# Six column groups of a conditioning projection: matmuls on TensorE replaced by product-sums on VectorE

## The chip, the cores and the metric

The kernel runs on one core of a Trainium2 chip. The metric is the device time of one execution in microseconds (us). A core has five engines, each with an instruction queue of its own that it takes in order: TensorE (PE, matrix multiply; PEld is its weight load), VectorE (DVE), ScalarE (ACT), GpSimd (POOL) and SyncE (SP, which here only issues transfers). They wait for each other by semaphores. Sixteen DMA engines move data between DRAM and the core's memory (SBUF); matmul results land in PSUM.

## The reference

One inference step of a two-layer trunk over 128 context tokens and 1024 latent tokens with 1024 features. The even layer runs neighbourhood attention beside a bidirectional gated linear attention (GLA), the odd layer window attention beside a DeltaNet; each layer ends in a convolutional FFN. Every sub-layer is shifted, scaled and gated by numbers that a projection of the conditioning vector gives:

```
def adaln(cond, w, b):
    return jnp.split(jax.nn.silu(cond) @ w + b, 6, axis=-1)
```

`cond` is one vector of 1024 for the context tokens and one for the latent tokens; `w` is 1024 by 6144 for each layer. So 2 x 6144 sums of 1024 products are needed for a layer. Nothing of it depends on the tokens.

## The kernel before

All activations lie with features on the 128 partitions and tokens along the free axis. Products of full precision are made by three passes (the weights and the activations are split into a high and a low part, `whi`, `wlo`, `hh`, `hl`; helper `gemm8`, L156 to L158).

The conditioning projection of the even layer has 6144 columns, that is 12 groups of 512 or 48 chunks of 128. Groups 0 to 3 are made at the start of the kernel, groups 4 to 9 during the linear attention (`even_b`), chunks 40 to 47 and all of the odd layer later on GpSimd and ScalarE (`ada_side`). `ada_groups` makes a group with eight matmuls (L208): silu(cond), 128 x 32, is the stationary side, a 128 x 512 piece of the weights (256 KB, tile `wada`, two buffers in `even_b`) the moving one. ScalarE copies the result (L211, `adarow`), four small matmuls turn it onto the partitions (L215), and VectorE adds the bias (L216).

`even_b` goes through four pairs of heads, p = 0 to 3. For each, `main(p)` runs the chunks of the recurrence: decay factors are multiplied onto keys and queries (L984, `kt` and `qt`, VectorE), each chunk's keys are transposed (L997, `ktr`, PE), copied out of PSUM (L999, `ktok`, VectorE), multiplied with the values (L1017, `u`, PE) and chained (L1005, VectorE); then come the attention inside a chunk (L1049 `att`, L1052, L1053) and the outputs (L1065, L1070 `ob`). Beside it `side(p)` yields the projections for pair p + 1 (`proj_b`, PE), its decay exponents (`zgen`, L910 to L932: `z` on PE, then ScalarE and VectorE) and the conditioning groups. A greedy weave lays them side by side in the program, and the framework's scheduler then sets the final order on each engine; in this part of the kernel no engine's order is written out by hand. Each engine's queue holds its instructions in that one order, transfers issued by SP included.

The line of `side(p)` for p < 3 is

```
yield from self.mix(proj(), self.ada_groups([(0, 4 + 2 * p), (0, 5 + 2 * p)], mp, 2), 1, 1)
```

The results are needed for the gate of the first sub-layer (chunks 16 to 23, when the output projection adds to the rows) and for the FFN's shift and scale (chunks 24 to 39).

Of the kernel before, what the change touches and what calls it, by code (L numbers as in the profile page):

```python
# [8 lines left out]
F32 = mybir.dt.float32  # L9
# [3 lines left out]
ALU = mybir.AluOpType  # L13
# [3 lines left out]
T = 1152  # L17
# [23 lines left out]
NEG = -1.0e30  # L41
# [11 lines left out]
class Net:  # L53
# [42 lines left out]
    def banks(self, g, m):  # L96
        """the banks of PSUM, until the stack is closed"""
        st = ExitStack()
        self.pg = st.enter_context(self.tc.tile_pool(name="pg", bufs=g, space=PSUM))
        self.pm = st.enter_context(self.tc.tile_pool(name="pm", bufs=m, space=PSUM))  # L100
        return st
# [22 lines left out]
    def pat(self):  # L124
        """either kind of bank, in turn"""
        self.turn = (self.turn + 1) % 8
        return self.pgt() if self.turn in (0, 3, 6) else self.pm.tile([128, 512], F32, name="g", tag="m")
# [34 lines left out]
    def proj(self, name, i, blocks, evict):  # L162
        """h @ a chunk of 128 columns; the next chunk of the plan is split meanwhile"""
        key = (name, i)
        if self.plan and self.plan[0] == key:
            self.plan.pop(0)
        if self.ahead is None or self.ahead[0] != key:
            self.ahead = (key, self.wchunk(self.I[name][i]))
        hi, lo = self.ahead[1]
        for b, (c0, n) in enumerate(blocks):  # L170
            ps = self.pgt()
            self.gemm8(ps, hi, lo, self.hh, self.hl, c0, n)
            if b == 0 and self.plan:
                self.ahead = (self.plan[0], self.wchunk(self.I[self.plan[0][0]][self.plan[0][1]]))
            evict(b, ps)
            yield 3.9

    def cond(self):
        nc = self.nc
        s = self.const("cond_s", [128, 8, 2])  # L180
        nc.sync.dma_start(s, self.I["condT"])
        self.nc.scalar.activation(s, s, AF.Silu)
        s4 = self.const("cond_s4", [128, 8, 32])
        nc.gpsimd.memset(s4, 0.0)
        nc.scalar.copy(s4[:, :, 0:2], s)
        self.s4 = s4

    def ada_groups(self, groups, pool, bufs):
        """silu(cond) @ ada_w for 512 columns each, the partial products in four column groups"""
# [13 lines left out]
        for l, g in groups:  # L203
            ps = self.pgt()
            for k in range(8):
                load()
                r = slice(32 * (k % 4), 32 * (k % 4) + 32)
                nc.tensor.matmul(ps[r, :], self.s4[:, k, :], ws.pop(0), start=(k < 4), stop=(k >= 4), skip_group_check=True)  # L208
                yield 0.6
            row = self.spool.tile([128, 512], F32, name="adarow", tag="part", bufs=1)  # L210
            nc.scalar.copy(row, ps)  # L211
            ps = None
            pt = self.pmt()
            for j in range(4):
                nc.tensor.matmul(pt[:, 2 * j:2 * j + 2], row[:, j * 128:(j + 1) * 128], self.sel42, start=True, stop=True)  # L215
            nc.vector.tensor_tensor(  # L216
                out=self.ada[l][:, 4 * g:4 * g + 4, :],
                in0=pt[:, 0:8].rearrange("p (a b) -> p a b", b=2),
                in1=self.adab[l][:, 4 * g:4 * g + 4].unsqueeze(2).to_broadcast([128, 4, 2]),
                op=ALU.add,  # L220
            )
            yield 0.4

    def ada_side(self, parts):
        """silu(cond) @ ada_w with the outputs on the partitions, for chunks of 128 columns: products on GpSimd, sums on ScalarE"""
# [61 lines left out]
    def weave(self, main, fill):  # L287
        """main yields how much of fill (us) to put in next, or None when it waits for fill"""
# [74 lines left out]
    def norm_row(self, x, l, w, b, k, r):  # L363
        """the modulated norm of a row in three steps, to lay between matmuls"""
# [28 lines left out]
    def slot(self, rate):  # L393
        """a step of each row under way, and of as many new ones as the rate says"""
# [8 lines left out]
    def norm_steps(self, b, t0, t1, row):  # L403
        """the norm of a block; its rows are left to slot()"""
# [9 lines left out]
    def blocks(self, x, order, gate, work, post, hook, rate, rate2, pool):  # L414
        """work(b, m) leaves what is to be added to row m of block b; the norm of a block goes on beside the next one's matmuls"""
# [34 lines left out]
    def scaled(self, t, x, l, w, b, k, r):  # L450
        """x over its norm; but for GpSimd's rows, also times the norm's gain and the scale"""
# [8 lines left out]
    def shifted(self, t, l, w, b, k):  # L460
        """plus the shift, in two parts"""
# [47 lines left out]
    def attn(self, mp, units, fill, depth=1):  # L509
        """units yields None (not ready) or a unit; three stages in flight, the first over depth units"""  # L510
# [103 lines left out]
    def even_gate(self, popen, I):  # L614
        """the first norm, modulated by halves of the rows as their shifts and scales come; silu of half of the linear attention's output gate"""
# [221 lines left out]
    def narrow(self, src, dst):  # L837
        """h @ w for 32 columns of w; dst(b, ps) gets [32, n]"""
# [13 lines left out]
    def even_b(self, mp):  # L852
# [48 lines left out]
        def zgen(p):  # L901
            """decay exponents, relative to the middle of each chunk"""
# [191 lines left out]
        def side(p):  # L1094
            if p < 3:
# [6 lines left out]
                yield from self.mix(proj(), self.ada_groups([(0, 4 + 2 * p), (0, 5 + 2 * p)], mp, 2), 1, 1)  # L1102
# [29 lines left out]
    def conv_ev(self, mp, w, dst):  # L1132
        """three-tap convolution; dst [128, T]"""
# [24 lines left out]
    def odd_1(self, mp, zp):  # L1158
# [26 lines left out]
        def gates():  # L1185
            """decay and write strength, per token: partition (head parity, token in chunk)"""
# [140 lines left out]
        def inv(p):  # L1327
            """inverse of the unit triangular 32 by 32 diagonal blocks, one system per partition"""
# [33 lines left out]
        def proj_c(i):  # L1362
            """a chunk for the window attention; but for the values, also with the rotated halves exchanged"""
# [71 lines left out]
    def odd_2(self, mp, zp):  # L1435
# [29 lines left out]
        def merge(p, d):  # L1465
            """inverse of the unit triangular blocks of 64"""
# [126 lines left out]
    def odd_3(self, pp, x):  # L1593
# [73 lines left out]
        def post(cs, small):  # L1667
            """norm and gate of six chunks; returns them by features"""
# [160 lines left out]
    def mix(self, a, b, na, nb):  # L1829
        """na steps of a, then nb of b, and so on"""  # L1830
# [12 lines left out]
    def split_t(self, dst, k, t):  # L1843
        """a row block of the mixers' output, in two parts"""
# [18 lines left out]
    def out_half(self, l, qs, row, then, done=None, later=None):  # L1863
        """output projection of the first mixer: adds to two rows of x for each of qs"""
# [37 lines left out]
    def out_rest(self, l, x, ws, order, hook):  # L1902
        """output projection of the second mixer, and the norm that follows"""
# [13 lines left out]
    def ffn_first(self, l, b, m):  # L1917
        """the first weights of the FFN, ahead of it"""
        j = FG[0][0]
        if (b, m) in ((l ^ 1, 0), (2, 3)):  # L1920
            self.first.append(self.wchunk(self.I["ffnup"][l, 2 * j + 1 - len(self.first)]))

    def ffn(self, l, x, start, hook, side=None, steps=None):
# [3 lines left out]
        with tc.tile_pool(name=f"ffn{l}", bufs=2) as fp:  # L1927
# [87 lines left out]
            def down_block(g, ws, i, b):  # L2015
                """ws: chunks of weights, of which the parts from i on are used"""
# [78 lines left out]
def mask_a():  # L2095
    """additive mask (0 or NEG) of a strip of 8 columns against the strips around it; order (column, row)"""
# [41 lines left out]
def outchunks(w):  # L2138
    """[half of the rows][pair of column blocks][128, (column block, row block, column)]"""
# [185 lines left out]
```

## Time and profile before

| | |
|---|---|
| runs | 3506.6, 3506.62 and 3512.47 us, median 3506.62 |
| span of the profiled execution | 3510.8 us |
| PE busy | 96% of the span |
| DVE, ACT, POOL busy | 56%, 41%, 23% |
| the linear attention's first three pairs | about 458 to 720 us |

The profile gives no time of the profiled execution besides its span, which lies between the lowest and the highest of the runs. Busy time counts instructions that compute; waits and issues of transfers are not in it. PEclk is the granted clock of TensorE as a share of full speed. In a chain of waits each piece is what the next one had to wait for, so a piece's length is time that the end of the kernel hung on.

### The profile page before, as it was taken

The page shows a single profiled execution, that of the slowest core. Times are in us where ns is not written, and L with a number is a line of the kernel's source. Part 1 is how long each engine was busy: PE and PEld are TensorE (multiplying, and loading weights), DVE is VectorE, ACT ScalarE, POOL GpSimd, SP SyncE. Part 2 cuts the span into 40 slices and gives each one's busy share as a digit, 9 for nine tenths or more (in the row PEclk, how much of TensorE's full clock was granted, in tenths as well). Part 3 has the DMA queues.
Part 4 walks back from the last instruction along what each step waited for, and adds up shares of the span by engine and source line. Part 5 has one row for each costly group of instructions (what it writes and reads, how often), then busy time and mean ns, then how long its engine had stood idle before and what let it go on. Part 6 is the DMA issues. An engine that isn't in the chain of part 4 may idle for free.

```text
span 3510.8 us, 58537 instructions
## 1 busy us (share of the span) xinstructions
PE 3355.3 (96%) x23239; PEld 3074.0 (88%) x23239; DVE 1975.3 (56%) x3848; ACT 1432.3 (41%) x3265; POOL 802.3 (23%) x1064
## 2 busy tenths in 40 slices
PE   6999999999999999999899877999999999999997
PEld 4988777779999999999798776677889999999997
DVE  5354444456655555555757776655676454445556
ACT  4355444444644444443554444541254222212223
POOL 1000010002544544451306676002310000000002
PEclk9999999999999999999999988999999999999999
DMA  5211122243222222221213454206511111111111
GB/s 197 85 49 49 54 62 84 84 161 129 77 84 80 83 76 86 82 88 52 84 57 106 123 135 131 52 15 205 164 46 29 41 42 41 41 44 43 43 43 66
DMA packets 182523, 282.04 MB, mean 80 GB/s; under 512 B 81867, under 2 KB 126027, under 8 KB 182124
## 3 DMA queue, kind: packets, MB, share of 16 engines
q1 hardware_dynamic: 151084, 224.88, 20.7%
q10 hardware_dynamic: 27184, 38.68, 3.8%
q0 software_dynamic: 3984, 14.75, 1.5%
q8 instruction: 184, 3.01, 0.4%
q14 instruction: 87, 0.71, 0.1%
HBM read 229.89 MB, written 48.37 MB: 79 GB/s over the span
## 4 chain that ended last, share of the span: by engine, by line
PE 81%; POOL 6%; DMA 4%; DVE 4%; ACT 2%; issue 2%; SPq 1%; DVEq 0%; POOLq 0%; ACTq 0%
PE g L156 14%; PE g L157 14%; PE g L158 14%; PE g L2025 5%; PE g L2023 5%; PE g L2024 5%; PE g L1860 4%; POOL sysN L1357 3%; POOL syst L1355 2%; PE s L507 2%; PE s L506 2%; PE ptr L595 2%; PE pvo L606 2%; PE g L208 2%; PE kqs L1631 1%
## 5 line engine op out<-in xcount | busy, mean ns | idle before, releaser
L156 PE MATMUL g<-hh,whi 128*128 128x386 f32 (+2 forms) x3264 | 1123.2, 344 | 18.6 <-ACT df L1373 11.2
L157 PE MATMUL g<-hl,whi 128*128 128x386 f32 (+2 forms) x3264 | 1113.5, 341 | 1.7 <-DVE hl L389 1.7
L158 PE MATMUL g<-hh,wlo 128*128 128x386 f32 (+2 forms) x3264 | 1109.2, 340 | 5.2 <-DVE wlo L144 5.1
L156 PEld LDWEIGHTS g<-hh,whi 128*128 128x128 f32 x3264 | 620.3, 190 | 41.0 <-issue 20.2
L157 PEld LDWEIGHTS g<-hl,whi 128*128 128x128 f32 x3264 | 619.3, 190 | 10.8 <-issue 6.8
L158 PEld LDWEIGHTS g<-hh,wlo 128*128 128x128 f32 x3264 | 618.7, 190 | 7.0 <-DVE wlo L144 5.9
L1933 ACT ACTIVATE u<-g,cw 128x384 f32<-128x384 f32 (+1 forms) x264 | 153.9, 583 | 769.8 <-PE g L158 769.8
L1934 DVE SCALAR_TENSOR_TENSOR u<-g,cw,u 128x384 f32<-128x384 f32 (+1 forms) x264 | 163.2, 618 | 528.9 <-ACT u L1933 528.6
L481 DVE SCALAR_TENSOR_TENSOR x<-g,ada,x 128x128 f32<-128x128 f32 (+1 forms) x608 | 294.7, 512 | 205.3 <-PE g L2025 190.9
L141 ACT CAST whi<-wraw 128x1024 fp32r<-128x1024 f32 (+2 forms) x202 | 201.1, 995 | 459.3 <-PE g L2024 238.7
L2024 PE MATMUL g<-gl,whi 128*128 128x384 f32 (+1 forms) x1008 | 341.4, 339 | 1.9 <-DVE gl L1989 1.9
L2023 PE MATMUL g<-gh,whi 128*128 128x384 f32 (+1 forms) x1008 | 342.7, 340 | 0.2
L2025 PE MATMUL g<-gh,wlo 128*128 128x384 f32 (+1 forms) x1008 | 342.4, 340 | 0.0
L144 DVE TENSOR_TENSOR wlo<-wraw,whi 128x1024 fp32r<-128x1024 f32 (+2 forms) x214 | 256.2, 1198 | 118.8 <-ACT whi L141 118.6
L262 POOL TENSOR_TENSOR adat<-wada,adas 128x384 f32<-128x384 f32 x168 | 174.7, 1040 | 318.9 <-DMA wada<-in_adaw 279.1
L2024 PEld LDWEIGHTS g<-gl,whi 128*128 128x128 f32 x1008 | 190.8, 189 | 2.4 <-issue 2.4
L262 POOL TENSOR_TENSOR wada<-wada,adas 128x384 f32<-128x384 f32 x168 | 189.0, 1125 | 13.2
L2023 PEld LDWEIGHTS g<-gh,whi 128*128 128x128 f32 x1008 | 190.7, 189 | 0.8 <-issue 0.8
L2025 PEld LDWEIGHTS g<-gh,wlo 128*128 128x128 f32 x1008 | 189.9, 188 | 0.0
L1970 POOL MEMSET gh<- 128x1 f32 x44 | 4.3, 100 | 782.0 <-PE g L2025 777.5
L1935 DVE SCALAR_TENSOR_TENSOR u<-g,cw,u 128x384 f32<-128x384 f32 (+1 forms) x264 | 163.3, 619 | 9.3
L1860 PE MATMUL g<-hh,whi 128*128 128x384 f32 (+1 forms) x384 | 117.1, 371 | 10.5 <-DVE x L481 4.7
(363 smaller groups left out, 4952.6 us busy)
## 6 DMA issues: line engine op xcount, KB each, us to landing
wraw<-in_ffnup SPq DMA_DIRECT2D x88, 512.0 KB
wada<-in_adaw ACTq DMA_DIRECT2D x112, 192.0 KB
wada<-in_adaw SPq DMA_DIRECT2D x80, 256.0 KB
wraw<-in_wi SPq DMA_DIRECT2D x38, 512.0 KB
kq<-kq_dram SPq DMA_DIRECT2D x36, 512.0 KB
wraw<-in_ffndn SPq DMA_DIRECT2D x40, 384.0 KB
wada<-in_adaw ACTq DMA_DIRECT2D x56, 128.0 KB
wraw<-in_wi ACTq DMA_DIRECT2D x12, 512.0 KB
```

Of the source, the lines that this page charges most:

```text
L141: nc.scalar.copy(hi[:, :n], raw[:, :n])
L144: nc.vector.tensor_tensor(out=lo[:, c], in0=raw[:, c], in1=hi[:, c].bitcast(F32), op=ALU.subtract)
L156: mm(ps[:, :n], w, ah[:, k, c0:c0 + n], start=(k == 0), stop=False)
L157: mm(ps[:, :n], w, al[:, k, c0:c0 + n], start=False, stop=False)
L158: mm(ps[:, :n], lo[:, k * 128:(k + 1) * 128], ah[:, k, c0:c0 + n], start=False, stop=(k == 7))
L262: nc.gpsimd.tensor_tensor(out=d[:, :m], in0=w[:, :m], in1=sb[:, j, sl], op=ALU.mult)
L481: nc.vector.scalar_tensor_tensor(out=xr[:, t:t + nn], in0=ps[:, o:o + nn], scalar=gate[:, m, j:j + 1], in1=xr[:, t:t + nn], op0=ALU.mult, ...
L1860: mm(ps[:, :n], a[:, w], src[:, 2 * k + j, c0:c0 + n], start=(k + x == 0), stop=(k + x == 5))
L1935: nc.vector.scalar_tensor_tensor(out=t, in0=ps[:, 2:n], scalar=w[:, 2:3], in1=t, op0=ALU.mult, op1=ALU.add)
L2023: mm(ps[:, :n], hi[:, o:o + 128], gh[:, c0:c0 + n], start=(s == 0), stop=False)
L2024: mm(ps[:, :n], hi[:, o:o + 128], gl[:, c0:c0 + n], start=False, stop=False)
L2025: mm(ps[:, :n], lo[:, o:o + 128], gh[:, c0:c0 + n], start=False, stop=(s == ng - 1))
```

## The change

Groups 4 to 9 (chunks 16 to 39) are made by `ada_rows` on VectorE: one instruction multiplies a 128 x 512 piece of the transposed weights (outputs on the partitions, half of the 1024 inputs along the free axis) with silu(cond), spread over all partitions, and adds up the products into one number per partition. Each piece is used twice, for the two conditioning vectors; the second time the products overwrite the piece. Eight chunks go with each pair of heads: first their first halves, then their second. The weights' buffers stay at two. silu(cond) goes to DRAM at the start and comes back spread (`csb`, 512 KB for each half, one buffer). Three small tiles change their pool.

```diff
     def cond(self):
         nc = self.nc
-        s = self.const("cond_s", [128, 8, 2])
+        s = self.gp.tile([128, 8, 2], F32, name="cond_s", tag="cond_s", bufs=1)
         nc.sync.dma_start(s, self.I["condT"])
         self.nc.scalar.activation(s, s, AF.Silu)
-        s4 = self.const("cond_s4", [128, 8, 32])
+        self.cs_dram = self.dr.tile([1, 2, 1024], F32, name="cs_dram")
+        for j in range(2):
+            nc.scalar.dma_start(self.cs_dram[0, j].rearrange("(k p) -> p k", p=128), s[:, :, j])
+        s4 = self.gp.tile([128, 8, 32], F32, name="cond_s4", tag="cond_s4", bufs=1)
...
+    def ada_rows(self, l, c0, c1, pool):
+        nc = self.nc
+        n = c1 - c0
+        todo = [(c, h) for h in range(2) for c in range(c0, c1)]
+        ws = []
+
+        def load():
+            if todo:
+                c, h = todo.pop(0)
+                w = pool.tile([128, 512], F32, name="wada", tag="wada", bufs=2)
+                nc.sync.dma_start(w, self.I["adaw2"][l, c, :, 512 * h:512 * h + 512])
+                ws.append(w)
+
+        load()
+        acc = pool.tile([128, 8, 2, 2], F32, name="adacc", tag="adacc", bufs=1)
+        for h in range(2):
+            sb = pool.tile([128, 2, 512], F32, name="csb", tag="csb", bufs=1)
+            nc.sync.dma_start(sb, self.cs_dram[:, :, 512 * h:512 * h + 512].to_broadcast([128, 2, 512]))
+            for c in range(n):
+                load()
+                w = ws.pop(0)
+                for j in range(2):
+                    t = pool.tile([128, 512], F32, name="adj", tag="adj", bufs=1) if j == 0 else w
+                    nc.vector.tensor_tensor_reduce(out=t, in0=w, in1=sb[:, j], scale=1.0, scalar=0.0,
+                                                   op0=ALU.mult, op1=ALU.add, accum_out=acc[:, c, j, h:h + 1])
+                yield 0.0
+        out = self.ada[l][:, c0:c1, :]
+        nc.vector.tensor_tensor(out=out, in0=acc[:, :n, :, 0], in1=acc[:, :n, :, 1], op=ALU.add)
+        nc.vector.tensor_tensor(out=out, in0=out, in1=self.adab[l][:, c0:c1].unsqueeze(2).to_broadcast([128, n, 2]), op=ALU.add)
+        yield 0.0
...
-                yield from self.mix(proj(), self.ada_groups([(0, 4 + 2 * p), (0, 5 + 2 * p)], mp, 2), 1, 1)
+                yield from self.mix(proj(), self.ada_rows(0, 16 + 8 * p, 24 + 8 * p, mp), 1, 2)
```

How the instructions stand. First VectorE where the recurrence of pair 0 begins: `wlo` is the low part of the next projection's weights, `qt` the queries, `ktok` the copies of the first two chunks' transposed keys. Before:

```order
L144 TENSOR_TENSOR wlo_4332<-wraw_4329,whi_4331 128x1024
L984 TENSOR_TENSOR qt_4294<-qt_4294,qf_3965 128x1152
L984 TENSOR_TENSOR qt_4296<-qt_4296,qf_3965 128x1152
L999 COPY ktok_4383<-ktr_4380 128x256
L999 COPY ktok_4388<-ktr_4385 128x256
```

And the same place now (the product-sums and the reads of their accumulator both show as ISA, `adacc` holds the sums):

```order
L251 ISA adacc_4346 128x1
L144 TENSOR_TENSOR wlo_4335<-wraw_4332,whi_4334 128x1024
L1019 TENSOR_TENSOR qt_4297<-qt_4297,qf_3968 128x1152
L1019 TENSOR_TENSOR qt_4299<-qt_4299,qf_3968 128x1152
L251 ISA adj_4721,adacc_4346<-wada_4716,csb_4595 128x512
L251 ISA adacc_4346 128x1
L251 ISA wada_4716,adacc_4346<-wada_4716,csb_4595 128x512
L251 ISA adacc_4346 128x1
L255 TENSOR_TENSOR ada0_93<-adacc_4346 128x16
L256 TENSOR_TENSOR ada0_93<-ada0_93,adab0_91 128x16
L1034 COPY ktok_4395<-ktr_4392 128x256
L1034 COPY ktok_4400<-ktr_4397 128x256
```

All 16 pieces of chunks 16 to 23 stand ahead of the first `ktok`, the last one between `qt` and `ktok`. The same place on PE, before (`g` is a projection's result, `ktr` the transposed keys, `u` the product that needs the first `ktok`):

```order
L997 MATMUL ktr_4380<-ident_73,kt_4295 128x128
L997 MATMUL ktr_4380<-ident_73,kt_4297 128x128
L997 MATMUL ktr_4385<-ident_73,kt_4295 128x128
L997 MATMUL ktr_4385<-ident_73,kt_4297 128x128
L208 MATMUL g_4343<-wada_4344,cond_s4_119 32x512
L156 MATMUL g_4413<-hh_131,whi_4236 128x384
L157 MATMUL g_4413<-hl_135,whi_4236 128x384
L1017 MATMUL u_4390<-vtb_3968,ktok_4383 64x64 x4
```

And now:

```order
L1032 MATMUL ktr_4392<-ident_73,kt_4298 128x128
L1032 MATMUL ktr_4392<-ident_73,kt_4300 128x128
L1032 MATMUL ktr_4397<-ident_73,kt_4298 128x128
L1032 MATMUL ktr_4397<-ident_73,kt_4300 128x128
L156 MATMUL g_4419<-hh_134,whi_4239 128x384
L157 MATMUL g_4419<-hl_138,whi_4239 128x384
L158 MATMUL g_4419<-hh_134,wlo_4240 128x384
L1052 MATMUL u_4402<-vtb_3971,ktok_4395 64x64 x4
```

The conditioning matmul is gone, and `u` still stands three matmuls behind the transposes. Last, VectorE ahead of pair 1's first `ktok`, before (`wlo`, `qt` and `ktok` as above):

```order
L144 TENSOR_TENSOR wlo_5015<-wraw_5012,whi_5014 128x1024
L984 TENSOR_TENSOR qt_4977<-qt_4977,qf_4300 128x1152
L984 TENSOR_TENSOR qt_4979<-qt_4979,qf_4300 128x1152
L999 COPY ktok_5086<-ktr_5083 128x256
L999 COPY ktok_5091<-ktr_5088 128x256
```

And now, the end of a run of product-sums that begins right behind `qt` (`oTb` is pair 0's output):

```order
L251 ISA adacc_5771 128x1
L251 ISA wada_5823,adacc_5771<-wada_5823,csb_5772 128x512
L251 ISA adacc_5771 128x1
L998 SCALAR_TENSOR_TENSOR oTb_4669<-oTb_4669,bng_3879,rsb_5091 128x1152
L251 ISA adj_5915,adacc_5771<-wada_5828,csb_5772 128x512
L251 ISA adacc_5771 128x1
L251 ISA wada_5828,adacc_5771<-wada_5828,csb_5772 128x512
L251 ISA adacc_5771 128x1
L251 ISA adj_5920,adacc_5771<-wada_5913,csb_5772 128x512
L251 ISA adacc_5771 128x1
L1034 COPY ktok_5152<-ktr_5149 128x256
L1034 COPY ktok_5157<-ktr_5154 128x256
```

These are product-sums of chunks 32 to 39, which the program yields beside pair 2's projections: they moved ahead of pair 1's recurrence.

## Rows read from the trace of the kernel before

**Rows 1.** The page's head and its busy time by engine.

```profile
span 3510.8 us, 58537 instructions
...
PE 3355.3 (96%) x23239; PEld 3074.0 (88%) x23239; DVE 1975.3 (56%) x3848; ACT 1432.3 (41%) x3265; POOL 802.3 (23%) x1064
```

**Rows 2.** Table by stretch: length, busy us (instructions) by engine, clock, DMA share, GB/s.

```profile
458.00:554.00 96.00, 95.71 (x616) 72.10 (x615) 42.90 (x73) 43.15 (x84) 8.80 (x10) 1.00 0.25 70
554.00:640.00 86.00, 85.87 (x552) 61.73 (x551) 37.10 (x68) 42.76 (x80) 7.47 (x10) 1.00 0.27 82
640.00:720.00 80.00, 79.87 (x517) 55.44 (x516) 34.01 (x68) 39.65 (x79) 7.47 (x10) 1.00 0.32 98
sum 262.00, PE 261.44 PEld 189.26 DVE 114.00 ACT 125.55 POOL 23.75; mean PE 87.15 PEld 63.09 DVE 38.00 ACT 41.85 POOL 7.92
```

**Rows 3.** Chain of waits, 430 to 720 us, shares by line.

```profile
by line: PE g L156 16.9%; PE g L157 16.3%; PE g L158 15.8%; PE g L208 14.2%; PE att L1049 6.2%; PE z L910 5.9%; PE ob L1070 5.1%; PE u L1017 3.6%; PE ob L1065 3.6%; PE ktr L997 2.9%; DMA wada<-in_adaw 2.7%; PE m L215 1.7%; PE vtr L895 1.4%;
```

**Rows 4.** Pieces of that chain: start us, us, engine, tile, line, count.

```profile
469.91 0.98 PE g L208 x2
...
477.27 0.38 PE u L1017 x8
...
512.25 1.05 PE m L215 x8
...
563.33 0.38 PE u L1017 x8
...
594.27 0.79 PE m L215 x8
...
604.87 3.88 DMA wada<-in_adaw
```

**Rows 5.** PE by line, 455 to 715 us: busy us, mean ns, idle before.

```profile
L208 PE MATMUL g<-wada,cond_s 128*32 128x512 f32 x96 | 46.0, 605 | 0.3
...
L215 PE MATMUL m<-sel,adarow 128*128 128x2 f32 x48 | 5.8, 244 | 0.3 <-ACT adarow L211 0.3
```

**Rows 6.** VectorE by line and shape, whole span; columns as in rows 5.

```profile
L561 DVE CUSTOM_DVE_ANT_0 sc<-s,bias 128x512 f32<-128x512 f32 x48 | 33.1, 690 | 42.2 <-PE s L507 41.7
...
L2087 DVE SCALAR_TENSOR_TENSOR x<-x,fing,rb 128x384 f32<-128x384 f32 x14 | 13.9, 1017 | 4.1 <-ACT rb L346 4.1
...
L561 DVE DVE_READ_ACCUMULATOR2_ANT mx<- 128x1 f32 x144 | 11.9, 83 | 0.0
...
L963 DVE SCALAR_TENSOR_TENSOR oTb<-oTb,bng,rsb 128x1152 f32<-128x1152 f32 x3 | 4.3, 1420 | 6.2 <-ACT rsb L962 6.2
```

**Rows 7.** VectorE in order of time, 452 to 500 us; idle before in brackets.

```profile
466.62 1.23 DVE L144 TENSOR_TENSOR wlo<-wraw,whi 128x1024 fp32r<-128x1024 f32 x1 [5.24 <-ACT whi L141]
467.76 2.62 DVE L984 TENSOR_TENSOR qt<-qt,qf 128x1152 f32<-128x1152 f32 x2
475.57 0.76 DVE L999 COPY ktok<-ktr 128x256 f32<-128x256 f32 x2 [5.18 <-PE ktr L997]
```

**Rows 8.** Chain of waits, 0 to 100 us: the first conditioning load.

```profile
16.42 3.21 DMA wada<-in_adaw
```

**Rows 9.** Table by stretch behind a wait of PE, columns as in rows 2.

```profile
736.00:740.00 4.00, 0.47 (x2) 0.50 (x3) 4.00 (x7) 1.07 (x2) 0.00 (x0) 0.84 0.72 224
740.00:744.00 4.00, 4.00 (x14) 4.00 (x14) 2.35 (x4) 1.25 (x2) 0.00 (x0) 0.50 0.47 192
744.00:748.00 4.00, 4.00 (x30) 3.29 (x30) 2.86 (x7) 0.52 (x2) 0.00 (x0) 0.81 0.52 147
```

**Rows 10.** ScalarE in order of time at the start.

```profile
17.41 0.22 ACT L182 ACTIVATE cond_s<-cond_s 128x16 f32<-128x16 f32 x1
```

**Rows 11.** Table by stretch at the start, columns as in rows 2.

```profile
20.00:30.00 10.00, 9.43 (x30) 2.69 (x28) 1.38 (x8) 0.48 (x1) 1.66 (x2) 0.94 1.01 358
```

**Rows 12.** Transfers, 2200 to 2300 us: packets, MB, share of 16 engines.

```profile
DMA packets 8572, 4.60 MB, mean 46 GB/s; under 512 B 7792, under 2 KB 7792, under 8 KB 8560
...
q1 hardware_dynamic: 8560, 4.43, 18.5%
```

More of the change, by code (lines that the diff above doesn't have):

```diff
@@ L209, in ada_groups @@
                 yield 0.6
-            row = self.spool.tile([128, 512], F32, name="adarow", tag="part", bufs=1)
+            row = self.gp.tile([128, 512], F32, name="adarow", tag="part", bufs=1)
             nc.scalar.copy(row, ps)
```

## Prediction

> **What bounds the kernel now.** Read first the page's busy line [rows 1]: TensorE (PE) is busy 96% of the 3510.8 us, VectorE (DVE) 56%. An average does not say what one stage is worth, so next comes the table by stage [rows 2], cut where the kernel goes from one pair of heads of the linear attention to the next: in its three stretches of 96, 86 and 80 us PE is busy 95.71, 85.87 and 79.87 us, at granted clock 1.00, and DVE only 42.90, 37.10 and 34.01. The chain of waits for the same part [rows 3] runs almost wholly over PE: an instruction taken off PE here is time off the end, as long as nothing makes PE wait instead. The pieces of that chain [rows 4] give what one costs: a conditioning matmul (L208, two passes) holds PE for 0.98 us, the eight passes of the small transposes that close a group (L215) for 1.05, elsewhere down to 0.79.
>
> **What is removed.** 48 conditioning matmuls of 0.975 us are 46.8 us, six closing transposes at about 0.85 are 5.1: 51.9 us of PE, which is the whole possible gain. The count agrees with the grouped rows, 96 passes and 48 passes [rows 5]. The six copies of the row on ScalarE and the six small adds on DVE go too and end nothing. The chain also lists 3.88 us of a load at 604.87; PE was working meanwhile (its stage was 85.87 of 86 us busy), so I give nothing for it.
>
> **What is added on DVE.** 24 column chunks in two halves are 48 pieces of 256 KB; each piece gets two product-sums of 128x512. The trace has this instruction with the same shape, in the first mixer's softmax: 690 ns plus 83 ns for the read of the accumulator [rows 6]. There one source lies in PSUM; here both lie in SBUF. Lower bound 0.62 us (the 83 ns and the tail lie under what follows), upper bound from the dearest row with two SBUF sources, 1017 ns for 384 elements, so 1.36 us for 512 [rows 6]. I take 0.77, nearest the row of the same instruction: 1.55 us a piece, 74 us in all. DVE has 262 − 114 = 148 us idle in the three stretches, so the work fits; the order decides whether it fits where it stands. [...]
>
> **Where it stands.** All 16 pieces of the first third come ahead of the first ktok copies in DVE's order, the next 16 and five and a half of the last third ahead of the second stage's ktok copies. So the work runs about a stage earlier than the matmuls did, and DVE is full up to about 570 us. PE needs ktok for its u matmuls, and DVE takes its queue in order.
>
> First ktok. Before, DVE did wlo at 466.62 and qt at 467.76 and then stood idle until PE's ktr released ktok at 475.57 [rows 7]: 5.24 us of idle time ahead of wlo and 5.18 ahead of ktok, 10.4 us in all. Now five pieces (7.7 us) stand there. Of these, one waits for its load: two buffers mean that a piece's load starts when the piece two ahead is done, 3.88 us to landing [rows 4] (3.21 at the start of the kernel [rows 8]), less the 1.55 us of the piece between: 2.3. Further up, the second half of the vector silu(cond) goes into a single buffer, so its load starts only after the last product-sum of the first half; with product-sums queued ahead of the decay steps, kt comes some 5 us late. 5 + 7.7 + 2.3 − 10.4 is 4.6, and PE arrives 1 us sooner without its L208 at 469.91: PE waits 5 to 8 us for ktok, at u (477.27 before).
>
> Second ktok. From the first to the second, DVE has its own 37.5 us (37.10 in 86 us [rows 2], over 87 us), 43 product-sums (33 us), seven places where a third piece follows two with little between (1.65 to 2.35 us each, 12 to 16 us) and one reload of silu(cond) (3.2 to 3.9 us): 86 to 90 us, starting 5 to 8 us after 475.6. That is 567 to 574. PE's u stood at 563.33 [rows 4]. I take 7 us late, and 2 to 14 as ends, since some of the load waits may lie under waits that DVE has anyway, or add to them. So the 18.3 us that PE had been relieved of by then (17 matmuls, two closings) are lost, and 7 more.
>
> From there on. 31 matmuls and four closings are still to go: 30.2 + 3.4 = 33.6 us. Product-sums left: 21, 16 us of DVE in a stage that has 37 us of its own against some 69 of PE (86 less 17), and none in the stage after. I charge 6 us (3 to 10): about 3 for att and z evictions queued behind product-sums, and 3 for the clock. [...] The last stage I charge 1 us.
>
> **The start.** Two stores of silu(cond) to DRAM are put on ScalarE's queue right after the silu at 17.41 [rows 10], each of 1,024 runs of four bytes. From 20 to 30 us the DMA engines are full (1.01) [rows 11] with the loads PE's first matmuls need, and the stores take two of the eight completion semaphores through which SP's loads go in turn, so an early load can wait for a store. A stretch of 8,572 packets, 7,792 of them under 512 bytes, took 18.5% of 16 engines over 100 us for its main queue [rows 12]: 35 ns of an engine each, so 2,048 packets are 4.5 us of all 16. Bounds 0 (under other loads) and 6 us; I take 3. Each reload of the vector is 512 KB, 3 MB in all, in stretches with DMA share 0.25 to 0.32: hidden but for the waits counted.
>
> **Sum.** 33.6 − 7 − 6 − 1 − 3 = 16.6, say 17 us. Taken from the profiled span of 3510.8 it gives 3494; that execution's span lies 4 us above the median of the runs, 3506.6, from which I take it: 3490.
>
> **Rivals.**
> The cover holds everywhere. If DVE is nowhere late, only the start is charged: 51.9 − 3 = 49, so 3458. For it: 148 us of idle DVE. Against: in-order waits for loads with two buffers, and 21 pieces ahead of one needed copy. Chance 0.08.
>
> Slower: product-sums from two SBUF sources run as the 1017 ns row does, at 1.36 us. This adds 0.67 us each: 10 ahead of the first ktok (6.7 us), 43 ahead of the second (29 us), and about 3 us in the third stage, where DVE then has 72 us against PE's 69. 39 − 17 = 22 us slower, 3529. It decides from about 0.98 us a product-sum on, where the 17 us are used up. Against: the 1420 ns row and the 690 ns row. Chance 0.12. [...]
>
> No change: relief given back. The second ktok 14 us late, 12 us lost in the third stage to evictions behind product-sums, the start 6: 33.6 − 33 is nothing, 3506. For it: the same interleaving stands in each stage. Chance 0.18.
>
> That the change would not take the matmuls off PE is excluded by the order of its instructions.
>
> **How the numbers follow.** My forecast has 0.62; with its own ends (second ktok 2 to 14, third stage 3 to 10, start 0 to 6) it covers 3478 to 3504. About 0.2%, 7 us, is what a measurement can tell from no change. Some 0.09 of the forecast lies within that of 3506.6. Faster: 0.53 + 0.08 = 0.61. Same: 0.09 and 0.13 of the third rival, 0.22. Slower: 0.12 and 0.05 of the third rival, 0.17. The range that leaves 2 in 10 outside reaches into both sides: 3470 to 3516.
>
> **What would show it.** Right: no L208 in these stages; the product-sum near 690 ns; PE waiting 5 to 8 us at the first ktok and several at the second, with a granted clock of 0.50 behind; DVE waiting for wada loads some 2 us at a time; no such waits in the last stage, which is about 20 us shorter than before; the first conditioning matmuls about 3 us later. Wrong: a product-sum above 0.98 us, a first u not later than its matmuls allow, or a stage after the second ktok in which PE waits more than 10 us.

## The result and the profile after

The changed kernel takes 3488.48 us (median of 4 runs, 3488.36 to 3488.96), the kernel before 3508.41 us (4 runs, 3506.6 to 3512.47): ratio 0.9932, 95% interval 0.9913 to 0.9952, so 17 to 31 us faster. 3490 us had been predicted. The medians differ by 19.9 us and the two profiled spans by 3510.8 - 3485.9 = 24.9 us: before's span is longer than three of its four run times, so its profile shows the slowest of them, and some 5 us of the 24.9 may belong to that choice of run and not to the change. The head of the changed kernel's page, which answers to [rows 1]:

```profile
span 3485.9 us, 58431 instructions
...
PE 3321.6 (95%) x23095; PEld 3074.4 (88%) x23095; DVE 2035.4 (58%) x4040; ACT 1427.7 (41%) x3259; POOL 810.3 (23%) x1064
```

TensorE (PE) is busy 33.7 us less, not the 51.9 that were taken from it, and VectorE (DVE) 60.1 us more. Where the rest went is seen in a table by stage. The cuts are the first z matmul, the first ktok copy of each of the four pairs, and the last ob matmul. First before, then after (columns: stretch, its length, PE busy with its instructions, granted clock, DMA share, GB/s):

```profile
425.40:475.60 50.20, 50.20 (x268) 1.00 0.14 44
475.60:562.60 87.00, 86.71 (x558) 1.00 0.24 69
562.60:649.20 86.60, 86.47 (x556) 1.00 0.27 83
649.20:740.40 91.20, 85.21 (x542) 0.97 0.44 140
740.40:796.40 56.00, 56.00 (x428) 0.95 0.38 127
```

```profile
433.90:484.70 50.80, 49.72 (x269) 1.00 0.39 122
484.70:569.00 84.30, 78.84 (x532) 0.92 0.34 109
569.00:645.50 76.50, 74.28 (x502) 0.91 0.24 76
645.50:717.30 71.80, 68.00 (x466) 0.90 0.35 115
717.30:773.70 56.40, 55.70 (x431) 0.97 0.43 146
```

Three things stand in these rows. The first z comes 8.5 us later: the start is dearer than it was. The whole stretch is 31.2 us shorter (339.8 against 371.0). And the granted clock, 1.00 in the first two stages of before, is 0.92, 0.91 and 0.90: PE waits little, but part of what is left to it runs at a lower granted clock, 0.50 where it is lowest (528 to 532 us, in the slices below). The stretch is split below into PE's idle time, its clock loss (PE busy times one minus the granted clock, summed over 60 equal slices) and the work at full clock that is left. Work fell from 360.0 to 305.6 us, so the relief of 51.9 was there; idle rose from 6.4 to 13.2, clock loss from 4.6 to 20.9. A stretch of low clock is called a dip below.

**The start.** In the changed kernel SyncE's queue (SP) waits for the two small stores, and the DMA engines, full in before [rows 11], stand mostly idle meanwhile. Its longest wait from 14 to 50 us (who waits, for what: us in total, times, longest):

```profile
SPq L201 <- DMA cs_dram<-cond_s: 10.9, 1, 10.9
```

In the traces of both kernels SP's issues up to 26 us carry eight semaphores in all, and from the ninth on each waits for the transfer that last carried its own. The two stores, issued at 17.74 and 18.16 us, carry two of these eight. SP's next load carries the first store's: the issue before it ends at 18.05, that store's last signal comes at 28.94, and the load is issued at 28.96. Issuing its first sixteen weight loads took 10.10 us before (first line) and takes 19.77 now:

```profile
16.42 10.10 SPq L198 DMA_DIRECT2D wada<-in_adaw  x16
16.67 19.77 SPq L201 DMA_DIRECT2D wada<-in_adaw  x16
```

The stretch of [rows 11] now (the last two columns are the DMA share and GB/s):

```profile
20.00:30.00 10.00, 5.82 (x9) 1.06 (x9) 0.52 (x3) 0.48 (x1) 0.00 (x0) 0.85 0.20 24
```

The stores' own packets are cheap. From 14 to 50 us their queue has 2,080 packets, which took 3.7% of the 16 engines' time, 1.3 us of all sixteen:

```profile
q10 hardware_dynamic: 2080, 0.01, 3.7%
```

**The product-sums** (duration in ns, least, median and most):

```profile
L251 DVE DVE_READ_ACCUMULATOR2_ANT adacc<- x96: 72/81/87, 428.8 to 626.1; 128x1 f32 x96
L251 DVE CUSTOM_DVE_ANT_0 adj<-wada,csb x48: 674/685/985, 428.2 to 624.8; 128x512 f32<-128x512 f32 x48
L251 DVE CUSTOM_DVE_ANT_0 wada<-wada,csb x48: 665/691/1142, 429.0 to 625.5; 128x512 f32<-128x512 f32 x48
```

685 and 691 ns with both sources in SBUF, against 690 for the same instruction with other operations (add and maximum) and one source in PSUM [rows 6]. VectorE's busy time rose by 60.1 us with the 96 of them, 0.63 each: in a row they start as little as 0.61 us apart.

**The waits of PE** from 420 to 800 us:

```profile
PE u L1052 <- DVE ktok L1034: 8.0, 5, 2.1
PE ob L1100 <- POOL at L1088: 2.5, 2, 1.6
PE z L945 <- DVE E L947: 1.1, 1, 1.1
PE vtr L930 <- DVE at L1087: 1.0, 1, 1.0
```

8.0 us of them, in five waits, are for ktok, the kind that was forecast, though each is short. The first is the one ahead of the first u (start, duration, idle before):

```profile
485.18 0.45 PE L1052 MATMUL u<-vtb,ktok 128*64 128x64 f32 x8 [1.57 <-DVE ktok L1034]
```

The others are new: PE waits for GpSimd's and VectorE's steps of the attention and of the decay, where before, with conditioning matmuls in between, it waited for none of these. Behind some of these waits the clock fell, here to 0.50. The second half of the first stage, in slices of 4 us:

```profile
516.00:520.00 4.00, 4.00 (x46) 1.00 0.53 197
520.00:524.00 4.00, 3.45 (x24) 1.00 0.37 131
524.00:528.00 4.00, 3.00 (x16) 0.67 0.16 57
528.00:532.00 4.00, 4.00 (x24) 0.50 0.38 129
532.00:536.00 4.00, 4.00 (x20) 0.55 0.05 17
```

From 528 to 536 PE is busy all the time at about half its clock, after waits of 0.2, 0.3 and 1.1 us from 521 to 525. What PE ran from 515.5 to 531.5 us, grouped by line (count, busy, mean ns, idle before):

```profile
L1084 PE MATMUL att<-qt,kt 64*128 64x128 f32 x38 | 5.0, 314 | 0.2 <-DVE at L1087 0.2
L1105 PE MATMUL ob<-qt,ss 64*64 64x128 f32 x32 | 3.5, 357 | 0.0
L945 PE MATMUL z<-glr,wz 33*128 33x384 f32 x6 | 3.1, 606 | 1.1 <-DVE E L947 1.1
L1100 PE MATMUL ob<-at,vtb 128*64 128x128 f32 x20 | 2.7, 358 | 0.0
L930 PE MATMUL vtr<-ident,vfb 128*128 128x128 f32 x9 | 2.0, 340 | 0.3 <-ACT vtb L931 0.3
L158 PE MATMUL g<-hh,wlo 128*128 128x384 f32 x1 | 0.3, 332 | 0.0
```

One projection matmul (`g`) in 16 us; the rest are short ones or ones on part of the array. In before, the same steps of the attention (502.5 to 518.5 us) had projection and conditioning matmuls among them, and the clock stayed at 1.00:

```profile
L1049 PE MATMUL att<-qt,kt 64*128 64x128 f32 x32 | 3.4, 285 | 0.0
L157 PE MATMUL g<-hl,whi 128*128 128x384 f32 x9 | 3.1, 345 | 0.0
...
L208 PE MATMUL g<-wada,cond_s 128*32 128x512 f32 x4 | 2.1, 604 | 0.0
```

The gaps ahead of this fall are waits for VectorE and ScalarE, the longest of 1.1 us. Such a gap alone does not decide: at the first ktok of this kernel PE waited 1.6 us among projection matmuls, and the clock stayed at 1.00 from 480 to 492; it fell behind the next wait, of 1.9 us, to 0.83 from 492 to 496 and 0.74 from 496 to 500.

**The second ktok.** VectorE's instructions from 562 to 570 us (start, duration, what ended the idle time before):

```profile
562.22 0.69 DVE L251 CUSTOM_DVE_ANT_0 wada<-wada,csb 128x512 f32<-128x512 f32 x1
562.84 0.08 DVE L251 DVE_READ_ACCUMULATOR2_ANT adacc<- 128x1 f32 x1
565.67 1.42 DVE L998 SCALAR_TENSOR_TENSOR oTb<-oTb,bng,rsb 128x1152 f32<-128x1152 f32 x1 [2.74 <-ACT rsb L997]
567.00 0.69 DVE L251 CUSTOM_DVE_ANT_0 adj<-wada,csb 128x512 f32<-128x512 f32 x1
...
568.96 0.75 DVE L1034 COPY ktok<-ktr 128x256 f32<-128x256 f32 x2
```

and the same place before:

```profile
562.61 0.76 DVE L999 COPY ktok<-ktr 128x256 f32<-128x256 f32 x2 [8.24 <-PE ktr L997]
565.18 1.42 DVE L963 SCALAR_TENSOR_TENSOR oTb<-oTb,bng,rsb 128x1152 f32<-128x1152 f32 x1 [1.81 <-ACT rsb L962]
```

VectorE was not full here. It stood for ScalarE's rsb, with ktok queued behind oTb and three product-sums; before, ktok stood ahead of oTb. In the third stage it waits 9.6 us so. From the first to the second ktok VectorE was busy for 65.90 of 84.30 us, and of its idle time only this was for the loads of the product-sums (pieces, then silu(cond)):

```profile
484.70:569.00 84.30, 65.90 (x154) 0.92 0.34 109
DVE adj L251 <- DMA wada<-in_adaw: 4.4, 5, 1.3
DVE adj L251 <- DMA csb<-cs_dram: 2.4, 1, 2.4
```

### The profile page after: what moved, and what is told of

Same layout as the page of the kernel before. It is cut to its first block, busy times and chain, and to the rows that moved or that the text cites. A ratio compares the mean times of both kernels' runs of the same rounds, so it can differ in the third digit from the quotient of the medians.

```text
span 3485.9 us, 58431 instructions
## 1 busy us (share of the span) xinstructions
PE 3321.6 (95%) x23095; PEld 3074.4 (88%) x23095; DVE 2035.4 (58%) x4040; ACT 1427.7 (41%) x3259; POOL 810.3 (23%) x1064
## 4 chain that ended last, share of the span: by engine, by line
PE 79%; POOL 6%; DVE 5%; DMA 3%; issue 3%; ACT 2%; SPq 1%; DVEq 0%; POOLq 0%; ACTq 0%
PE g L156 14%; PE g L157 14%; PE g L158 14%; PE g L2060 5%; PE g L2058 5%; PE g L2059 5%; PE g L1895 4%; POOL sysN L1392 3%; POOL syst L1390 2%; PE s L542 2%; PE s L541 2%; PE ptr L630 2%; PE pvo L641 2%; PE kqs L1666 1%; PE g L1518 1%
## 5 line engine op out<-in xcount | busy, mean ns | idle before, releaser
L156 PE MATMUL g<-hh,whi 128*128 128x386 f32 (+2 forms) x3264 | 1126.8, 345 | 18.4 <-ACT df L1408 12.8
L156 PEld LDWEIGHTS g<-hh,whi 128*128 128x128 f32 x3264 | 623.3, 191 | 32.3 <-ACT df L1408 13.1
L297 POOL TENSOR_TENSOR wada<-wada,adas 128x384 f32<-128x384 f32 x168 | 190.1, 1132 | 13.2
```

The lines of the kernel that those rows point to most:

```text
L156: mm(ps[:, :n], w, ah[:, k, c0:c0 + n], start=(k == 0), stop=False)
L297: nc.gpsimd.tensor_tensor(out=d[:, :m], in0=w[:, :m], in1=sb[:, j, sl], op=ALU.mult)
```

## The experiments

Two theories of where the rest of the 51.9 us went. **A**: VectorE loses it; its product-sums and their loads make ktok late, and the stores the start. **B**: the removed matmuls were themselves the cover for the attention's waits (the work that PE did meanwhile), and the long matmuls among short ones that kept the clock up. On the three chips of the experiments the kernel before ran from 3501 to 3534 us, more widely than on the first, so the lengths from the profiles carry the reading, and the ratio to before on the same chip stands beside them. Lengths in us; "stretch" is first z to last ob.

| kernel | first z | stretch | PE idle | clock loss | ratio to before, 95% |
|---|---|---|---|---|---|
| before | 425.4 | 371.0 | 6.4 | 4.6 | 1 |
| changed | 433.9 | 339.8 | 13.2 | 20.9 | 0.9932 (0.9913 to 0.9952) |
| late_stores | 438.4 | 336.5 | 14.5 | 15.9 | 0.9923 (0.9901 to 0.9945) |
| stores_behind | 422.4 | 333.2 | 11.5 | 16.2 | 0.9901 (0.9874 to 0.9928) |
| before_stores | 436.2 | 370.6 | 6.4 | 4.4 | 1.0034 (1.0020 to 1.0049) |
| relief_only | 420.6 | 332.7 | 8.0 | 19.7 | 0.9871 (0.9828 to 0.9913) |
| relief_spread | 422.2 | 313.5 | 6.9 | 2.6 | 0.9837 (0.9816 to 0.9859) |
| before_spread | 420.3 | 371.4 | 9.0 | 4.0 | 1.0007 (0.9993 to 1.0021) |
| spread | 433.3 | 331.0 | 15.8 | 10.6 | 0.9911 (0.9884 to 0.9938) |
| both | 422.0 | 332.3 | 15.7 | 12.2 | 0.9891 (0.9866 to 0.9916) |
| early_ktok | 424.6 | 329.9 | 15.4 | 8.9 | 0.9885 (0.9864 to 0.9906) |
| one_sum | 436.7 | 340.4 | 14.4 | 21.5 | 0.9951 (0.9930 to 0.9971) |
| w3_inplace | 433.0 | 336.9 | 13.2 | 17.3 | 0.9945 (0.9926 to 0.9964) |
| mix11 | 435.0 | 343.1 | 31.7 | 6.0 | 0.9958 (0.9938 to 0.9978) |

The changed kernel, late_stores and stores_behind have the same instructions in this stretch, and it took 339.8, 336.5 and 333.2 us: with product-sums, differences under some 7 us in one profile are not read. The kernel before, before_stores and before_spread lie within 0.8 us of each other. Each length is from one profile; the ratios of most kernels overlap.

**late_stores.**

```diff
...
-        for j in range(2):
-            nc.scalar.dma_start(self.cs_dram[0, j]..., s[:, :, j])
+        self.cs = s
...
     def even_gate_rest(self):
...
+            self.nc.scalar.dma_start(self.cs_dram[0, p - 2]..., self.cs[:, :, p - 2])
```

> The changed kernel, but the two stores of silu(cond) are issued some 60 us later, after the first conditioning groups, beside the last two chunks of the output gate. Theory A: these stores are what makes the first weight loads late, and all of the 8.5 us by which the changed kernel reaches its first linear-attention projection later (433.9 against 425.4 us); then 3488.5 - 8.5 = 3480 us, and PE's first conditioning matmuls stand where they stood before. Theory B: the delay comes from the other places in memory of the vector and its padded copy, or from the order at the start; then 3488 us, within 2.

It tested nothing: the scheduler put the stores back at 17.5 us, and the first z was as late as before the edit, or later (438.4). Written later is not issued later; inside the stretch whose order is written out by hand it is (the next one).

**stores_behind.**

```diff
...
-        for j in range(2):
-            nc.scalar.dma_start(self.cs_dram[0, j]..., s[:, :, j])
+        self.cs = s
...
                         nc.sync.dma_start(self.br_dram[i], ts[i])
+            for j in range(2):
+                nc.scalar.dma_start(self.cs_dram[0, j]..., self.cs[:, :, j])
             ps = ts = ws = None
```

> The changed kernel with the two stores of silu(cond) behind the first two output gates on ScalarE's queue, where they are held by the order written out by hand (in the first try they were still issued at 17.5 us). Theory A (a store's completion holds back the weight loads behind it): SP issues its first 16 weight loads in about 10 us, as before (19.8 in the changed kernel), the first z matmul comes at 425 us in place of 433.9, and the time is 3488.5 - 8.5 = 3480 us. Theory B (other places in memory, other order): first z at 434, 3488 us.

As theory A had it. The first z came at 422.4, 11.5 us earlier, and the median was 3479.28 us; the interval of its ratio overlaps that of the changed kernel, so the time alone would not show it. The sixteen issues are short again:

```profile
16.46 9.66 SPq L200 DMA_DIRECT2D wada<-in_adaw  x16
```

**before_stores**, the same from the other side.

```diff
         self.nc.scalar.activation(s, s, AF.Silu)
+        self.cs_dram = self.dr.tile([1, 2, 1024], F32, name="cs_dram")
+        for j in range(2):
+            nc.scalar.dma_start(self.cs_dram[0, j]..., s[:, :, j])
```

> The kernel before with the two stores of silu(cond) at the start and nothing else; nobody reads them. If the stores hold back the weight loads behind them, SP takes about 20 us for its first 16 weight loads (10.1 before), the first z comes 8 to 13 us later than 425.4, and the time is 8 to 11 us above before's. If the delay in the changed kernel came from elsewhere, no difference.

The stores alone make the first z 10.8 us late and the time 0.34% longer (12 us; 7 to 17 by the interval), with the same wait in SP's queue:

```profile
SPq L201 <- DMA cs_dram<-cond_s: 13.1, 2, 12.1
```

So the cost of the start is settled: some 8 to 13 us of SP's loads queued behind a store of 4 KB. Over the fourteen profiles the first z stands at 420.3 to 425.4 us in the seven without early stores and at 433.0 to 438.4 in the seven with them.

**relief_only.**

```diff
-                yield from self.mix(proj(), self.ada_groups([(0, 4 + 2 * p), (0, 5 + 2 * p)], mp, 2), 1, 1)
+                yield from proj()
...
+        nc.gpsimd.memset(self.ada[0][:, 16:40], 0.0)
```

> The kernel before with the six groups left out and nothing put in their place: the conditioning values of column groups 4 to 9 are set to zero, so the output is not the reference's. Theory A (VectorE loses the rest): without product-sums PE keeps the whole 51.9 us, 3508.4 - 51.9 = 3456.5 us, the recurrence is 52 us shorter than before (the changed kernel: 32). Theory B (the removed matmuls were themselves the cover for other waits, for POOL's and ScalarE's steps of the attention, and the clock falls behind such waits): the recurrence is shorter by about the same 32 us as in the changed kernel, and without stores at the start the time is 3476 us; the clock is low at the same two or three places.

Theory A alone falls by the profile. With no product-sum and no store the stretch is 38.3 us shorter, not 52, and the clock loss is 19.7 us, as large as in the changed kernel. The time alone would not say so: by the interval it is 31 to 60 us shorter. Theory B had expected 32, so both are tested further. PE's busy time over the whole stretch, and the granted clock:

```profile
420.60:753.30 332.70, 324.74 (x2200) 0.94 0.21 69
```

**spread** lays long matmuls among the short ones.

```diff
+            pq = self.proj("wi0", 12 + p, IB, evict(qf, 0.125))
             for g in range(3):
+                yield next(pq)
                 pt = self.pmt("vtr")
...
-            yield from self.proj("wi0", 12 + p, IB, evict(qf, 0.125))
+            for _ in pq:
+                pass
```

> The changed kernel with one edit in the order: each of the three groups of transposes of v (vtr) comes behind a block of the q projection (24 full matmuls) in place of all three ahead of it, so that long matmuls lie among the short ones of the attention (att, ob, z, vtr) in the second half of each stage. Product-sums and loads stay. Theory B (the rest is lost to the clock, which falls where the removed matmuls had been the only long ones): the 21.0 us of clock loss in the recurrence fall to 5 to 10, 3488.5 - 13 = 3475 us. Theory A (VectorE's queue): waits for ktok stay at 8 us and the time at 3488 us, within 3.

Half as expected. The clock loss fell from 20.9 (16 in the two profiles with the same stretch) to 10.6, but idle rose to 15.8, among it 5.9 us in the third stage for an hh copy of ScalarE that had been hidden. Long matmuls nearby did not always keep the clock up: behind a wait of 1.1 us it stood at 0.50 for some 9 us, in which PE ran 14 projection matmuls.

```profile
534.00:538.00 4.00, 4.00 (x22) 0.50 0.32 113
538.00:542.00 4.00, 4.00 (x13) 0.50 0.17 63
```

The median is 3483.6 us, and the ratio's interval overlaps those of the kernels without the edit.

**relief_spread**, the same edit without product-sums.

> The kernel before with the six groups left out (their values set to zero, the output is not the reference's) and the transposes of v dealt out between the blocks of q. No product-sum, no store. If the 19.7 us of clock loss that the kernel without the groups shows come from stretches that hold only short matmuls, they fall to 10 us or less here, and the recurrence (first z to last ob) from 332.7 to about 322 us. If the clock falls for another reason (waits alone, or the chip at that moment), it stays near 20 us and 333 us.

The clock loss is gone:

```profile
422.20:735.70 313.50, 306.62 (x2198) 0.99 0.22 74
```

19.2 us less than without the edit (332.7), all but 2 of them clock. The whole relief is there: 371.0 - 313.5 = 57.5 us. The median is 3456.56 us. So with the projection's matmuls dealt out among the short ones the clock no longer fell (loss 2.6 us, 19.7 without the edit). Which of theory B's two halves does it is not shown: ahead of the fourth pair's ktok relief_only has 4.9 us of waits for steps of the attention and the decay, and here they are gone as well, so the clock may have stayed up because the waits were covered.

**before_spread.**

> The kernel before with only the transposes of v dealt out between the blocks of q; its conditioning matmuls stay. If the removed matmuls were what kept the clock up in the second half of the stages, nothing is to be had here: clock loss stays near 4.6 us and the time at before's, within 4 us. If the order of the transposes were a gain by itself, 8 to 10 us below.

No difference in time or stretch; clock loss 4.0. The edit has no worth of its own: it does for the kernel without the groups what their matmuls had done.

**one_sum.**

```diff
-                for j in range(2):
-                    t = pool.tile([128, 512], ..., tag="adj", bufs=1) if j == 0 else w
+                for j in range(1):
+                    t = w
...
```

> The changed kernel with one of the two product-sums of each piece: the second batch gets the first's value, so the output is not the reference's. All loads stay. 48 product-sums less are 37 us of VectorE. Theory A (VectorE's queue is what makes PE wait): about half of the 20 us that are lost in the recurrence come back, 3478 us. Theory B (cover lost on PE): 3488 us, within 3, with PE's waits at the same places.

37 us less on VectorE brought nothing that can be measured. VectorE's waits for the pieces grew from 8.0 us to

```profile
DVE wada L251 <- DMA wada<-in_adaw: 25.3, 16, 4.6
```

What a piece with one sum cost ahead of a ktok copy was here largely its load, up to 4.6 us: PE's longest wait for ktok was 6.4 us.

**w3_inplace.**

```diff
-                w = pool.tile([128, 512], F32, name="wada", tag="wada", bufs=2)
+                w = pool.tile([128, 512], F32, name="wada", tag="wada", bufs=3)
...
```

> The changed kernel with three buffers for the pieces in place of two; for their room the first product-sum writes over its piece, and the second reads that, so the output is not the reference's. Theory A: the 8.0 us that VectorE waits for pieces go, and with them up to 5 us of PE's waits for ktok: 3484 us. Theory B: these waits lie where VectorE waits for ScalarE anyway, or the clock decides: 3488 us, within 2.

Not told apart. VectorE's waits for pieces fell from 8.0 to 2.4 us, PE waits 7.7 us for ktok in place of 8.0, and the stretch of 336.9 us lies within what the same kernel shows.

**mix11.**

```diff
-                    yield from self.mix(pr, zgen(p + 1), 1, 2)
+                    yield from self.mix(pr, zgen(p + 1), 1, 1)
```

> The changed kernel with the decay steps of the next pair dealt out one for each block of the projection in place of two. They end behind the q projection. Theory B (clock): z matmuls lie farther apart, clock loss falls from 21.0 us by about 8; the decay of the second direction comes some 10 us later, of which a few us may show as a wait at the next stage's first kt: 3480 to 3488 us. Theory A (VectorE late): the decay steps now end closer to the ktok copies, so waits for ktok grow by 5 us or more at each stage: 3500 us.

The clock loss fell to 6.0 as theory B had it, and was paid for elsewhere, more dearly than theory B said: idle rose by 18.5 us. The time is near theory A's 3500 us, but not by its way: the waits for ktok are 9.2 us in place of 8.0. The decay steps end too late, and PE waits for kt.

```profile
PE ktr L1032 <- DVE kt L1019: 16.9, 3, 11.6
```

In the middle of the second stage PE waited 1.5 us among short matmuls and projection matmuls (32 projection matmuls in 14 us), and here the clock did not fall:

```profile
590.00:594.00 4.00, 3.63 (x33) 1.00 0.65 199
594.00:598.00 4.00, 2.89 (x31) 1.00 0.42 108
```

**both** (stores_behind and spread together).

> The changed kernel with both edits: stores behind the gates, and transposes of v between the blocks of q. If both causes are right and add up: 3488.5 - 8.5 - 13 = 3467 us, below both kernels. If only the stores count: 3480 us; only the order: 3475 us; neither: 3488 us.

Median 3476.58 us (3469.85 to 3483.42), below both kernels, though not the 3467 of two full gains: beside stores_behind (3479.28, same chip) spread adds nothing that can be measured. The stretch:

```profile
422.00:754.30 332.30, 316.66 (x2200) 0.95 0.35 113
```

**early_ktok** (both, and ktok ahead of oTb).

```diff
-            for i in range(4):
+            for i in range(5):
                 yield next(c)
             if self.bpost is not None:
```

> The kernel with both edits (stores behind the gates, transposes spread), and the step with a stage's first ktr, ktok and u ahead of the norm of the pair before. In VectorE's order the first four ktok copies of the second and third stage then come ahead of oTb, which waits up to 9.6 us for ScalarE. If PE's waits at the second and third ktok hang on that, these go (some 3 us), and with them the dips of the clock behind (some 3 us): 5 us below the kernel with both edits, 3471 us. If the product-sums ahead of ktok decide, no difference from it, within 3 us.

Median 3471.93 us, the lowest of the kernels that leave nothing out; by its ratio it can't be told from both. The way from the first to the second ktok fell from 78.3 to 72.9 us, as asked, and the whole stretch by 2.4 us, which one profile does not tell from nothing.

**What the four corners say**, by the stretches of the kernels with and without product-sums, with and without the spread order. Groups out, spread (relief_spread): 313.5 us. Product-sums added to that (both): 332.3, so they cost 18.8 us (8.8 idle, 9.6 clock). Spread taken away instead (relief_only): 332.7, so the lost cover costs 19.2 (1.1 idle, 17.1 clock). Both at once, the changed kernel and its like: 333 to 340, 20 to 26 us and not 38. Each alone is enough to bring dips of the clock, though not all at the same places, and mending one alone gives little back. Whether the 18.8 us come from the sums themselves or from their loads stays open: one_sum and w3_inplace changed VectorE's waits, not the length.

## Why the prediction was right

The time, 3490 against 3488.5, is right, and so are the side and the cause of the gain: matmuls off the engine that bounds this part, with a part of the relief lost again. Where it is lost was forecast only in part; several terms are off and largely cancel. By the medians 19.9 us came where 16.6 were summed. The terms are read from the profiles, where 24.9 came; those of 2 us are less than one profile tells:

- **Relief.** 51.9 us; measured 54.4 at full clock (360.0 - 305.6). Right.
- **Product-sum.** 0.77 us; 0.685 to 0.691 plus 0.081. Right for one by itself; in place it was 0.63 of busy time, near the lower bound of 0.62, so 60 us in all and not 74. The slower rival (1.36 us) is out: 691 ns against 690 with a PSUM source.
- **First ktok.** PE was to wait 5 to 8 us. It waited 1.6 ahead of the first u and 3.4 in all from 480 to 496. The wait is there, so the prediction's sign of being wrong (a first u not later than its matmuls allow) did not come, but the size was too large. PE's own ktr came only at 482.5, so most of VectorE's pile lay under it; ktok is 9.1 us later than before, of which the start had made 8.5.
- **Second ktok**, 7 us late. It came 6.4 late, of which the start had made 8.5: 2.1 early by itself, 9 us better than the term. "DVE is full up to about 570 us" is wrong: it was idle for 18.4 of the 84.3 us from the first ktok to the second, and at the end stood for ScalarE behind oTb. The term that was mis-sized is the loads: 12 to 16 us for pieces and 3.2 to 3.9 for silu(cond) were summed, 4.4 and 2.4 measured. Most of what the first stage lost on PE is clock (0.92 over 84.3 us) and waits of 5.5 us; the sum had no clock there.
- **From there on** 33.6 - 6 - 1 = 26.6 us were to be gained, 204.7 against 233.8 is 29.1. The size is right, the reason too narrow. The charge of 1 us for the stage without product-sums rests on VectorE alone; there too the clock was low (0.90 from 645.5 to 717.3). relief_only, without any product-sum, lost 19.7 us of clock over the whole stretch (0.52, 0.50 and 0.70 in the slices from 508 to 520), so the lost cover is enough to bring such dips. The last two stages together are 19.0 us shorter (147.2 to 128.2), near the 20 forecast; they came out better for before's own 6.0 us of waits from 649 to 740, of which 3.8 are left.
- **The start**, 3 us with 6 as the most: 8.5, and 8 to 13 in other profiles. This term left its bounds too (those of the second ktok were 2 to 14 late). The mechanism had been named (an early load waits for a store); the bound was worked out from packet time [rows 12], which is the engines' time and not the wait of those queued behind. The stores' packets took 1.3 us of all sixteen engines where 4.5 were reckoned, and SP still waited 10.9 us; what holds their end back so long is not shown.
- **After the recurrence** 2.2 us more were gained, not forecast; whether the change did that or the run is open.

9.1 + 2.5 - 5.5 + 2.2 = 8.3 us, the difference between 24.9 and 16.6. That the time is so near is in part luck: the pessimism at the second ktok paid for the start. The base, taken 4.2 us under before's span, and the 2.6 us by which the changed kernel's run time lies above its span took up the rest but 1.5.

What was not in the prediction at all is that a removed matmul has a use beside its result: it covers waits between short matmuls, and where it was gone the clock fell, to 0.50 at its lowest. Whether it also keeps the clock up by itself stays open. The prediction charged 3 us for the clock in the third stage, about the dip from 740 to 748 us in [rows 9] (4 x 0.50 + 4 x 0.19 = 2.8 us); there were six dips, and the clock loss was 16.3 us above before's.

## What to carry to other kernels

Before work is taken off the busiest engine, look at what stands around it: if it is what fills the waits of a chain of short steps, part of its time can come back as waits and as a lower clock (here 6.8 and 16.3 us of the 51.9), and other long work has to be laid there first (clock loss 2.6 us in relief_spread, 19.7 in relief_only). A mended cause shows its worth only where no second one brings dips too (the spread order took 19.2 us off the stretch without product-sums, 0.9 from stores_behind to both), so try both together and each alone. A small scattered store early in a program is priced by who waits for its end, not by its bytes (here SP waited 10.9 us for one of 4 KB).

## What the runs showed of the hardware

Two stores of 4 KB, each in 1,024 runs of four bytes, held another queue's loads for 10.9 us in the changed kernel and 13.1 in before_stores, while the DMA share from 20 to 30 us, 1.01 before, was 0.20 and 0.15. The granted clock stood at 0.50 in slices in which PE was busy 4.00 of 4.00 us (528 to 532 in the changed kernel), behind waits of no more than 1.1 us among short matmuls. Such waits did not always bring it: 1.5 us in mix11 left the clock at 1.00. A product-sum of 128x512 f32 took 685 and 691 ns with both sources in SBUF, the same instruction 690 with one in PSUM.
